# A chunked recurrence cut into five parts, with merging work behind every burst

## The chip, the cores and the metric
One Trainium2 chip, one core of it. The metric is device time in microseconds of one execution; the median of three runs counts. Lower is better.

## The reference, cut to what matters
Two transformer blocks run one behind the other, each with two layers, on 512 positions of 1024 channels in fp32. The change lies in the first block, whose layers have four branches, of which one is a recurrence (RWKV-7), and then merge the branches:

```python
def step(state, inp):                      # for each of 512 positions, 8 heads of 64
    r_t, w_t, k_t, v_t, a_t, b_t = inp
    sa = jnp.einsum('bhvk,bhk->bhv', state, a_t)
    state = (state * w_t[:, :, None, :] + sa[..., None] * b_t[:, :, None, :]
             + v_t[..., None] * k_t[:, :, None, :])
    return state, jnp.einsum('bhvk,bhk->bhv', state, r_t)
...
branches = jnp.stack([y_rwkv, y_mla, y_conv, y_mem], axis=2)
proj = jnp.einsum('bsnc,ncd->bsnd', branches, w_o_branch[l])
gates = jax.nn.sigmoid(merge.reshape(B, S, N_BRANCH, D) + b_gate[l])
merged = jnp.sum(gates * proj, axis=2)
out = merged @ w_out[l]
x = _layer_norm(DEEPNORM_ALPHA * x + out, ln_g[l], ln_b[l])
```

The second block needs modulation vectors, a product of a vector with a 1024 x 6144 matrix for each of its layers (`w_ada`). VectorE computes it in the background, the one for layer 0 during the first block's recurrences, the one for layer 1 during the second block's first feed-forward.

## The kernel before, in words
Every large product is three matmuls of 512 columns on split weights (a high and a low part, `wh` and `wl`): high by high, high by low, low by high. Weights come in 512 KB pieces on SyncE's (SP's) DMA queue into two staging buffers (`wst`), and ScalarE (cast, line 204) and VectorE (subtraction, line 181) split them. The modulation's pieces (line 1270) use the same two staging buffers and the same queue.

**The recurrence** (`rwkv`) works on four pairs of heads (j), each in two halves (g) of four chunks of 64 positions: eight units u = 2j + g in a layer. For a pair, `prep` makes r, k, v and the decays (three products of 24 matmuls each, and small ones). For a unit, `solve` makes the triangular matrices of its chunks (AB, AK, by products of AR and BK), inverts them, and transposes BK. The inversion takes the 8x8 diagonal blocks through HBM into another layout (`tri`, `BL`), inverts them by substitution on VectorE (`sub`, 14 small operations), takes them back through HBM (into `stk`, lines 653 and 661) and then doubles the block size in three levels. A level is a product with AD, an evacuation into X under a mask, a product with X, an addition and a transposition (lines 676 to 699). `chain` then runs through the four chunks one after another: z from the state, two half copies of z into `rbd` (VectorE, then ScalarE, lines 722 and 723), a product with AB, two half copies into `ubd`, a product with BT that gives the next state (`sbd`), and a product with AB that gives the output. Behind every pair the output is normalized and gated.

**The order.** All three are generators, and `together` steps the chain of unit u, the solve of unit u + 1 and, for g = 0, the prep of pair j + 1 side by side in nine rounds. Between the steps `spread` issues the filler: units of merging work (`merge`, `gates`) of the other three branches and the gates of the first, 280 units a layer. Of 24 output blocks each takes 24 matmuls for its gate in eight units and 12 for its projection in a ninth; 8 further gates take 24 matmuls in eight units. `tick2` (once a round) advances the modulation by one step, which is four VectorE operations on half a piece for one of two vectors. The generator for layer 0 (`ada(0)`) has 120 steps.

What the text issues is a list; a planner in the framework turns it into one fixed order for each engine's queue when the program is built, by its own estimate of when operands and buffers are ready, with the text's order as priority. Weight loads are moved ahead in it. On the chip each queue then runs in its fixed order, and an instruction that waits holds what stands behind it on its engine. SP's queue holds the weight loads and the DMAs of `tri`, `BL` and `stk`.

Of the kernel before, what the change touches and what calls it, by code (L numbers as in the profile page):

```python
# [19 lines left out]
P = 128  # L20
KB, PB, VB, QB, A2, NF = 3, 6, 1, 3, 4, 2
RW = 1, 2
# [8 lines left out]
TW = (0.4, 1.4) + (1,) * 7  # L31
SHARE = {1: (1,), 2: (0.5, 0.5), 3: (0.5, 0.4, 0.1)}
W0 = 0.85
# [96 lines left out]
class K:  # L130
# [386 lines left out]
    def rwkv(self, l, st):  # L517
# [19 lines left out]
        for t in (*sbd, rbd, ubd, *vbd, BK, lora):  # L537
            nc.gpsimd.memset(t, 0.0)
# [71 lines left out]
        def solve(j, g):  # L610

            col = lambda v: cv[:, v + j:v + j + 1]
            r, k, v, Pd, Pi, pc, th, kk, bon = pre[j]
            bon = bon[:, 256 * g:256 * g + 256]
            r, k, v, Pd, Pi, th, kk = [t[:, 256 * g:256 * g + 256] for t in (r, k, v, Pd, Pi, th, kk)]
            pc = pc[:, 4 * g:4 * g + 4]
            AR = pool.tile([P, 4, 2, C], F32, name="AR", tag="AR", bufs=2)
            self.tt(AR[:, :, 0, 1:C], ch(kk)[:, :, 1:C], ch(Pd)[:, :, 0:C - 1], ALU.mult)
            nc.vector.tensor_copy(out=AR[:, :, 0, 0:1], in_=ch(kk)[:, :, 0:1])
            self.stt(kk, th, 1.0, kk, ALU.add, ALU.mult)  # L620
# [3 lines left out]
            self.tt(AR[:, :, 1, :], ch(r), ch(Pd), ALU.mult)  # L624
# [4 lines left out]

            AB, AK = [pool.tile([P, 4, P], F32, name=e, tag=e, bufs=2) for e in ("AB", "AK")]  # L630
            for e, t in enumerate((AB, AK)):
# [6 lines left out]
            d1, d2 = [t[g] for t in self.tri]  # L638
            for h in range(2):
                nc.sync.dma_start(out=d1[4 * h:4 * h + 4, 0:4096].rearrange("u (k i) -> k u i", k=C),  # L640
                                  in_=AB[hd[h], :, 0:64])
            BL = pool.tile([8 * C // NB, NB, NB], F32, name="BL", tag="BL")
            nc.sync.dma_start(out=BL, in_=diag(d1))
            AD = W("AD").rearrange("p (c m) -> p c m", c=4)
            nc.gpsimd.memset(AD, 0.0)
            for b in range(4):
                nc.scalar.copy(out=AD[blk[b], :, blk[b]], in_=A1(b, b % 2, b % 2))
            for i in range(1, NB):
                t = sub[1][:, 0:i, 0:i]
                self.tt(t, sub[0][:, 0:i, 0:i].rearrange("p k q -> p q k"),  # L650
                        BL[:, 0:i, i].unsqueeze(1).to_broadcast([8 * C // NB, i, i]), ALU.mult)
                nc.vector.tensor_reduce(out=sub[0][:, i, 0:i], in_=t, axis=AX.X, op=ALU.add)
            nc.sync.dma_start(out=diag(d2), in_=sub[0])


            stk = pool.tile([P, 2, 4, 32], F32, name="stk", tag="stk")
            T, TT = stk[:, 0], stk[:, 1]
            flat = lambda t: t.rearrange("p c d -> p (c d)")
            src = d2[:, 0:4096].rearrange("(h c) (k i) -> h k c i", h=2, k=C)
            for b in range(4):  # L660
                nc.sync.dma_start(out=T[blk[b]], in_=src[b // 2, blk[b % 2], :, blk[b % 2]])
            nc.vector.transpose(out=flat(TT), in_=flat(T))
            yield
# [9 lines left out]
            for e in range(2):  # L673
                for h in hd:
                    nc.scalar.copy(out=vb[h, :, e, h], in_=ps[hd[e], :, h])
            for lv in range(L0, 5):
                if lv == 4:
                    for b in range(4):
                        nc.scalar.copy(out=A1(b, b % 2, b % 2), in_=TT[blk[b]])
                        if b % 2:  # L680
                            nc.gpsimd.memset(T[blk[b]], 0.0)
                        else:
                            nc.scalar.copy(out=AD[blk[b], :, blk[b + 1]], in_=A1(b, 0, 1))
                ps = self.psum([P, 4, 32], "tp")
                for c in range(4):
                    self.mm(ps[:, c, :], AD[:, c, :], T[:, c, :], True, True)
                X = self.tmp.tile([P, S], F32, name="X", tag="t", bufs=self.tb).rearrange(
                    "p (c b d) -> p c b d", c=4, b=4)
                self.tt(X, ps.unsqueeze(2).to_broadcast([P, 4, 4, 32]),
                        lvl[:, lv - L0:lv - L0 + 1].to_broadcast([P, 4, 4, 32]), ALU.mult)  # L690
                ps = self.psum([P, 4, 32], "tp")
                for c in range(4):
                    self.mm(ps[:, c, :], X[:, c].rearrange("p b d -> p (b d)"), TT[:, c, :], True, True)
                if lv == 4:
                    for b in (0, 2):
                        nc.scalar.copy(out=A1(b, 0, 1), in_=ps[blk[b]])
                else:
                    self.tt(TT, TT, ps, ALU.add)
                    nc.vector.transpose(out=flat(T), in_=flat(TT))
                if lv == L0:  # L700
                    bk = BK.rearrange("p c a b -> p c (a b)")
                    self.tt(bk, bk, pc.to_broadcast([P, 4, 2 * P]), ALU.mult)
                    BT = pool.tile([P, 2, 4, P], F32, name="BT", tag="BT", bufs=2)
                    for e in range(2):
                        ps = self.psum([P, 4, P], "aux")
                        for q in range(4):
                            self.tr(ps[:, q, :], BK[:, q, e, :])
                        nc.scalar.copy(out=BT[:, e], in_=ps)
                yield
            solved[j, g] = AR, AB, AK, BT, pc  # L710

        def chain(j, g):


            col = lambda v: cv[:, v + j:v + j + 1]
            AR, AB, AK, BT, pc = solved[j, g]
# [8 lines left out]
            for q in range(4):  # L725
                c = 4 * g + q
                S0, S1 = sbd[c % 2], sbd[(c + 1) % 2]
                z = self.psum([P, P], "yb")
                self.mm(z, AK[:, q, :], vbd[g][:, q, :], True, c == 0)
# [4 lines left out]
                nc.scalar.copy(out=y, in_=z[64:128, :])  # L734
                ps = self.psum([P, P], "aux")
                self.mm(ps, AB[:, q, :], rbd, True, True)
                heads(ubd, ps)
                if c < NCH - 1:
                    ps = self.psum([P, P], "aux")
                    self.mm(ps, BT[:, 1, q, :], vbd[g][:, q, :], True, False)  # L740
                    self.mm(ps, BT[:, 0, q, :], ubd, False, True)
                    for b in hd:
                        if c:
                            self.stt(S1[b, b], S0[b, b], pc[b, q, :], ps[b, b], ALU.mult, ALU.add)
                        else:
                            nc.vector.tensor_copy(out=S1[b, b], in_=ps[b, b])
                ps = self.psum([P, P], "aux")
                self.mm(ps, AB[:, q, :], ubd, True, True)
                self.tt(y, ps[64:128, :], y, ALU.add)
                yield  # L750
                if q % 2:
                    yield
            if g == 0:
                return
# [1202 lines left out]
```

## Time and profile before

| | us |
|---|---|
| median of three runs | 3342.94 (3341.34 to 3352.66) |
| the profiled execution | 3355.74, span 3354.0 |
| TensorE matmul, busy | 3178.3 (95%) |
| VectorE, busy | 2295.1 (68%) |
| ScalarE, busy | 1272.6 (38%) |
| DMA | 310 MB, 92 GB/s in the mean |

Times in the rows count from the span's start. Matmuls are pipelined, so that their recorded durations overlap, and busy TensorE time is not time at its peak; the distance from one start to the next shows the pace. An fp32 product is recorded as two matmuls. The granted clock (PEclk) is the share of TensorE's full 2.4 GHz.

### The profile page before, as it was taken

The page shows a single profiled execution, that of the slowest core. Times are in us where ns is not written, and L with a number is a line of the kernel's source. Part 1 is how long each engine was busy: PE and PEld are TensorE (multiplying, and loading weights), DVE is VectorE, ACT ScalarE, POOL GpSimd, SP SyncE. Part 2 cuts the span into 40 slices and gives each one's busy share as a digit, 9 for nine tenths or more (in the row PEclk, how much of TensorE's full clock was granted, in tenths as well). Part 3 has the DMA queues.
Part 4 walks back from the last instruction along what each step waited for, and adds up shares of the span by engine and source line. Part 5 has one row for each costly group of instructions (what it writes and reads, how often), then busy time and mean ns, then how long its engine had stood idle before and what let it go on. Part 6 is the DMA issues. An engine that isn't in the chain of part 4 may idle for free.

```text
span 3354.0 us, 44202 instructions
## 1 busy us (share of the span) xinstructions
PE 3178.3 (95%) x16694; PEld 2658.2 (79%) x16694; DVE 2295.1 (68%) x4788; ACT 1272.6 (38%) x2300; POOL 98.0 (3%) x220
## 2 busy tenths in 40 slices
PE   8999899989999998999999899999999998999999
PEld 7877677777898776787778786888888887688887
DVE  8978678776779785776647878775464667964342
ACT  4445333332344462333433457422121234732221
POOL 0000000000000010000000000000000000000000
PEclk9999899988999998999989899999999999999999
DMA  5322233323453222333224321233242442123332
GB/s 174 89 65 62 81 89 91 111 70 94 145 147 82 56 65 70 97 86 81 60 66 126 113 75 43 90 109 111 83 125 89 145 124 88 43 76 93 102 95 88
DMA packets 438661, 310.06 MB, mean 92 GB/s; under 512 B 69025, under 2 KB 430545, under 8 KB 438449
## 3 DMA queue, kind: packets, MB, share of 16 engines
q1 hardware_dynamic: 431392, 292.60, 30.2%
q0 software_dynamic: 7056, 14.65, 1.7%
q8 instruction: 131, 2.15, 0.3%
q14 instruction: 82, 0.66, 0.1%
HBM read 295.13 MB, written 7.34 MB: 90 GB/s over the span
## 4 chain that ended last, share of the span: by engine, by line
PE 48%; DVE 9%; DMA 4%; ACT 3%; issue 1%; SPq 0%; ACTq 0%; POOL 0%; DVEq 0%
PE ps_mm L192 39%; PE ps_tp L192 2%; DVE wl L181 2%; PE ps_o L192 2%; DMA wst<-in_w_in_dram 1%; ACT wh L204 1%; PE ps_sc L192 1%; DMA wst<-in_w_gate_up_dram 1%; PE ps_aux L192 1%; DVE aacc L189 1%; PE ps_mx L192 1%; PE ps_yb L192 0%; DVE z L181 0%; PE ps_mx L196 0%; DVE h8l L189 0%
## 5 line engine op out<-in xcount | busy, mean ns | idle before, releaser
L204 ACT CAST wh<-wst 128x1024 fp32r<-128x1024 f32 (+3 forms) x453 | 458.6, 1013 | 1073.0 <-PE ps_mm L192 600.3
L181 DVE TENSOR_TENSOR wl<-wst,wh 128x1024 fp32r<-128x1024 f32 (+3 forms) x453 | 532.1, 1175 | 396.0 <-ACT wh L204 388.4
L192 PE MATMUL ps_mm<-xh,wh 128*128 128x512 f32 (+1 forms) x1200 | 497.3, 415 | 15.2 <-DVE rbd L722 3.8
L192 PE MATMUL ps_mm<-xl,wh 128*128 128x512 f32 (+1 forms) x1200 | 485.8, 405 | 0.0
L192 PE MATMUL ps_mm<-xh,wl 128*128 128x512 f32 (+1 forms) x1200 | 485.2, 405 | 0.0
L192 PE MATMUL ps_mm<-h8h,wh 128*128 128x512 f32 (+1 forms) x928 | 359.3, 388 | 6.6 <-ACT wh L204 4.9
L192 PE MATMUL ps_mm<-h8l,wh 128*128 128x512 f32 (+1 forms) x928 | 358.3, 387 | 0.1
L192 PE MATMUL ps_mm<-h8h,wl 128*128 128x512 f32 (+1 forms) x928 | 356.5, 385 | 2.0 <-DVE wl L181 2.0
L192 PEld LDWEIGHTS ps_mm<-xh,wh 128*128 128x128 f32 (+1 forms) x1200 | 231.6, 193 | 66.7 <-issue 5.7
L192 PEld LDWEIGHTS ps_mm<-xh,wl 128*128 128x128 f32 (+1 forms) x1200 | 230.8, 192 | 48.3 <-issue 0.7
L192 PEld LDWEIGHTS ps_mm<-xl,wh 128*128 128x128 f32 (+1 forms) x1200 | 231.5, 193 | 43.4 <-issue 0.7
L189 DVE SCALAR_TENSOR_TENSOR aacc<-wst,silc,aacc 128x256 f32<-128x256 f32 x560 | 250.2, 478 | 15.6 <-DMA wst<-in_w_ada_dram 11.3
L192 PEld LDWEIGHTS ps_mm<-h8h,wl 128*128 128x128 f32 x928 | 175.6, 189 | 39.1 <-DVE wl L181 3.6
L192 PEld LDWEIGHTS ps_mm<-h8h,wh 128*128 128x128 f32 x928 | 176.1, 190 | 28.6 <-ACT wh L204 6.1
L192 PEld LDWEIGHTS ps_mm<-h8l,wh 128*128 128x128 f32 x928 | 175.9, 190 | 20.5 <-DVE h8l L189 0.3
L192 PE MATMUL ps_mm<-fh,wl 128*128 128x512 f32 (+1 forms) x528 | 187.0, 354 | 2.1 <-DVE wl L181 2.1
L192 PE MATMUL ps_mm<-fl,wh 128*128 128x512 f32 (+1 forms) x528 | 187.7, 356 | 0.0
L192 PE MATMUL ps_mm<-fh,wh 128*128 128x512 f32 (+1 forms) x528 | 187.3, 355 | 0.0
L189 DVE SCALAR_TENSOR_TENSOR cacc<-ch,vec,cacc 128x512 f32<-128x512 f32 x240 | 168.6, 745 | 2.3 <-ACT cacc L178 1.8
L189 DVE SCALAR_TENSOR_TENSOR ft<-ft,ps_mm 128x512 f32<-128x512 f32 (+1 forms) x134 | 76.1, 586 | 115.3 <-PE ps_mm L192 66.3
L192 PE MATMUL ps_mm<-hch,wl 128*128 128x256 f32 x448 | 127.1, 284 | 1.5 <-DVE wl L181 1.5
L192 PE MATMUL ps_mm<-hcl,wh 128*128 128x256 f32 x448 | 126.7, 283 | 0.1
(547 smaller groups left out, 6456.1 us busy)
## 6 DMA issues: line engine op xcount, KB each, us to landing
wst<-in_w_in_dram SPq DMA_DIRECT2D x188, 512.0 KB, 3.9
wst<-in_w_ada_dram SPq DMA_DIRECT2D x96, 512.0 KB, 3.6
wst<-in_w_gate_up_dram SPq DMA_DIRECT2D x88, 512.0 KB, 3.9
wst<-in_w_out_dram SPq DMA_DIRECT2D x40, 512.0 KB, 3.5
wst<-in_w_down_dram SPq DMA_DIRECT2D x36, 512.0 KB, 3.4
wst<-in_w_o_branch_dram SPq DMA_DIRECT2D x32, 512.0 KB, 3.6
wst<-in_xattn_w_mem_kv_dram SPq DMA_DIRECT2D x16, 512.0 KB, 3.6
wst<-in_w_down_dram SPq DMA_DIRECT2D x20, 384.0 KB, 3.3
```

Of the source, the lines that this page charges most:

```text
L181: return self.nc.vector.tensor_tensor(out=out, in0=a, in1=b, op=op)
L189: return self.nc.vector.scalar_tensor_tensor(out=out, in0=a, scalar=s, in1=b, op0=op0, op1=op1)
L192: self.nc.tensor.matmul(out, lhsT=l, rhs=r, start=start, stop=stop)
L204: self.nc.scalar.copy(out=h, in_=src)
```

## The change
`solve` becomes four generators (or functions), and the output's normalization a fifth part of its own, `close`. A unit now runs: `triangles` of the next unit (5 bursts), the `chain` of this one (4 chunks of 3 bursts), and `doubling` of the next (3 levels of 4 bursts). The `substitute` step comes at the chain's third burst, the next `prep` at every second burst of the chain, `operands` of the unit after next at every second burst of the doubling, and `close` at every third. Behind every burst stands a `spot` of a weight (0.8 where a prep runs beside, 1.35 elsewhere), which issues filler through `drip` at a fixed rate, 280 units over a total weight of 281.95, and every second spot calls `tick2`. A layer has 248 spots.

Within the parts: doubling works on two pairs of chunks by turns; its last level has a tile AO of its own, instead of changing AD; AD and AO last, and are cleared once. X shares the buffer of `mx` instead of the temporaries; the square and the gate of `close` move to the temporaries. In the chain the product of BT with v is issued before the AB product, and the AK product with v of the next chunk at the end of this one. The modulation's generator yields once for both vectors, except in layer 0.

```diff
+    def drip(self, w):
+        self.debt += self.rate * w
+        while self.debt >= 1:
+            self.debt -= 1
+            self.tick()
...
-        def solve(j, g):
+        def operands(j, g):
...
+        def triangles(j, g):
...
             for e, t in enumerate((AB, AK)):
...
+                if e == 0:
+                    for h in range(2):
+                        nc.sync.dma_start(out=d1[4 * h:4 * h + 4, 0:4096].rearrange("u (k i) -> k u i", k=C),
+                                          in_=AB[hd[h], :, 0:64])
+                    nc.sync.dma_start(out=BL, in_=diag(d1))
+                yield
...
+        def substitute(j, g):
...
+            nc.sync.dma_start(out=diag(d2), in_=sub[0])
+            src = d2[:, 0:4096].rearrange("(h c) (k i) -> h k c i", h=2, k=C)
+            for b in range(4):
+                nc.sync.dma_start(out=stk[blk[b], 0], in_=src[b // 2, blk[b % 2], :, blk[b % 2]])
+
+        def doubling(j, g):
...
+            two = [slice(2 * i, 2 * i + 2) for i in range(2)]
+            for s in two:
+                nc.vector.transpose(out=flat(TT[:, s]), in_=flat(T[:, s]))
             for lv in range(L0, 5):
...
+                X = W("X", "mx").rearrange("p (c b d) -> p c b d", c=4, b=4)
+                for s in two:
+                    ps = self.psum([P, 2, 32], "tp")
+                    for c in range(2):
+                        self.mm(ps[:, c, :], (AO if lv == 4 else AD)[:, s.start + c, :], T[:, s.start + c, :], True, True)
+                    self.tt(X[:, s], ps.unsqueeze(2).to_broadcast([P, 2, 4, 32]),
+                            lvl[:, lv - L0:lv - L0 + 1].to_broadcast([P, 2, 4, 32]), ALU.mult)
+                    yield
+                for s in two:
+                    ps = self.psum([P, 2, 32], "tp")
...
+                        self.tt(TT[:, s], TT[:, s], ps, ALU.add)
+                        nc.vector.transpose(out=flat(T[:, s]), in_=flat(TT[:, s]))
+                    yield
...
+        def spot(w):
+            self.drip(w)
+            spots[0] += 1
+            if spots[0] % 2:
+                self.tick2()
+
+        def turns(w, main, *side):
+            for _ in main:
+                spot(w)
+                for t in side:
+                    next(t, None)
+            for t in side:
+                for _ in t:
+                    spot(w)
...
         for _ in prep(0):
-            self.spread(W0)
-        together(W0, solve(0, 0))
+            spot(0.5)
+        for _ in operands(0, 0):
+            pass
+        turns(1, triangles(0, 0))
+        for _ in operands(0, 1):
+            pass
+        for _ in range(4):
+            spot(2)
+        substitute(0, 0)
+        for _ in range(4):
+            spot(2)
+        turns(1, doubling(0, 0))
         for u in range(8):
...
             if u < 7:
+                turns(w, triangles(*nxt))
+                turns(w, chain(j, g), after(2, substitute, *nxt), *([every(2, prep(j + 1))] if more else []))
+                side = [every(2, operands((u + 2) // 2, (u + 2) % 2))] if u < 6 else []
+                turns(w, doubling(*nxt), *side, *([every(3, close(j))] if g else []))
+            else:
+                turns(w, chain(j, g))
+                turns(w, close(j))
...
-                    yield
+                    if l == 0 or v == vecs[-1]:
+                        yield
```

## Rows read from the trace of the kernel before

**Rows 1.** The page, the chain of waits by engine.
```profile
PE 48%; DVE 9%; DMA 4%; ACT 3%; issue 1%; SPq 0%; ACTq 0%; POOL 0%; DVEq 0%
```
**Rows 2.** Windows: stretch, length, busy (count) of PE, PEld, DVE, ACT, POOL, PEclk, DMA.
```profile
318.00:852.00 534.00, 484.17 (x2415) 402.24 (x2414) 383.42 (x998) 184.01 (x391) 13.26 (x39) 0.91 0.32 92
...
1252.00:1774.00 522.00, 486.55 (x2403) 403.41 (x2402) 326.36 (x836) 182.77 (x391) 13.04 (x38) 0.91 0.28 78
```
**Rows 3.** Waits of TensorE, 318 to 852: us in total, times, longest.
```profile
PE ps_tp L192 <- DMA stk<-tri: 18.6, 4, 9.5
PE ps_tp L192 <- DVE X L181: 5.3, 7, 1.2
PE ps_aux L192 <- ACT rbd L723: 3.7, 4, 2.1
PE ps_aux L196 <- DVE sub L181: 3.4, 1, 3.4
PE ps_tp L192 <- DVE stk L699: 2.6, 2, 1.8
```
**Rows 4.** Waits of TensorE, 1252 to 1774.
```profile
PE ps_tp L192 <- DMA stk<-tri: 11.6, 2, 9.5
PE ps_tp L192 <- DVE X L181: 7.3, 8, 1.6
PE ps_tp L192 <- DVE stk L699: 2.7, 3, 1.0
```
**Rows 5.** Windows at low clock (sums of six each), and the stretch between two.
```profile
sum 92.20, PE 69.11 PEld 60.08 DVE 44.58 ACT 20.94 POOL 2.51; mean PE 11.52 PEld 10.01 DVE 7.43 ACT 3.49 POOL 0.42
...
1366.30:1376.50 10.20, 10.18 (x39) 9.31 (x39) 4.35 (x13) 3.10 (x8) 0.00 (x0) 0.50 0.13 45
...
sum 88.70, PE 74.32 PEld 65.88 DVE 38.06 ACT 18.45 POOL 2.51; mean PE 12.39 PEld 10.98 DVE 6.34 ACT 3.07 POOL 0.42
...
386.60:475.40 88.80, 84.76 (x469) 71.21 (x468) 75.86 (x208) 33.65 (x77) 2.50 (x6) 1.00 0.36 101
```
**Rows 6.** TensorE in order of time: start, us, instruction.
```profile
384.24 0.63 PE L192 MATMUL ps_mm<-xh,wl 128*128 128x512 f32 x1
384.66 0.63 PE L192 MATMUL ps_mm<-xh,wh 128*128 128x512 f32 x1
...
396.00 0.48 PE L192 MATMUL ps_mm<-xh,wh 128*128 128x512 f32 x1
396.32 0.39 PE L192 MATMUL ps_mm<-xl,wh 128*128 128x512 f32 x1
396.55 0.39 PE L192 MATMUL ps_mm<-xh,wl 128*128 128x512 f32 x1
```
**Rows 7.** First substitution, first doubling product; a round of the chain.
```profile
365.09 0.15 DVE L181 TENSOR_TENSOR sub<-sub,BL 64x1 f32<-64x1 f32 x1
...
373.43 1.89 PE L192 MATMUL ps_tp<-stk,AD 128*128 128x32 f32 x8 [9.55 <-DMA stk<-tri]
...
714.29 0.49 PE L192 MATMUL ps_yb<-sbd,AR 128*128 128x128 f32 x2 [0.34 <-DVE sbd L189]
715.82 0.38 PE L192 MATMUL ps_aux<-rbd,AB 128*128 128x128 f32 x1 [1.04 <-ACT rbd L723]
```
**Rows 8.** VectorE: X by line, a tick, modulation in the second layer, its busiest stretch.
```profile
L181 DVE TENSOR_TENSOR X<-ps_tp,lvl 128x512 f32<-128x512 f32 x24 | 16.6, 691 | 31.3 <-PE ps_tp L192 31.0
...
342.07 1.92 DVE L189 SCALAR_TENSOR_TENSOR aacc<-wst,silc,aacc 128x256 f32<-128x256 f32 x4
...
1252.00:1774.00 522.00, 57.08 (x136) 0.91 0.28 78
...
1252.00:1774.00 522.00, 11.80 (x24) 0.91 0.28 78
...
84.00:168.00 84.00, 82.62 (x141) 1.00 0.34 88
```
**Rows 9.** Waits of TensorE, 2180 to 2690, in the second block's first feed-forward.
```profile
PE ps_mm L192 <- ACT wh L204: 4.9, 3, 2.1
```

More of the change, by code (lines that the diff above doesn't have):

```diff
@@ L536, in rwkv @@
         lora = pool.tile([P, 2, P], F32, name="lora")
-        for t in (*sbd, rbd, ubd, *vbd, BK, lora):
+        AD, AO = [pool.tile([P, 4, P], F32, name=e) for e in ("AD", "AO")]
+        stk = pool.tile([P, 2, 4, 32], F32, name="stk")
+        for t in (*sbd, rbd, ubd, *vbd, BK, lora, AD, AO):
             nc.gpsimd.memset(t, 0.0)
@@ L635, in solve @@
                 self.tt(t, ps, self.m_am.unsqueeze(1).to_broadcast([P, 4, P]), ALU.mult)
-            A1 = lambda b, q, e: AB[blk[b // 2 * 2 + q], :, blk[e]]
[L638 to L645, printed above, removed]
+                if e == 0:
[4 more added lines that the diff above has]
+                yield
+            A1 = lambda b, q, e: AB[blk[b // 2 * 2 + q], :, blk[e]]
             for b in range(4):
                 nc.scalar.copy(out=AD[blk[b], :, blk[b]], in_=A1(b, b % 2, b % 2))
[L648 to L662, printed above, removed]
-            yield
+                if b % 2 == 0:
+                    nc.scalar.copy(out=AO[blk[b], :, blk[b + 1]], in_=A1(b, 0, 1))
             self.stt(r, r, col(V_RK), k, ALU.mult, ALU.mult)
@@ L679, in solve @@
                         nc.scalar.copy(out=A1(b, b % 2, b % 2), in_=TT[blk[b]])
[L680 to L708, printed above, removed]
@@ new lines, in doubling @@
+                for s in two:
+                    ps = self.psum([P, 2, 32], "tp")
+                    for c in range(2):
+                        self.mm(ps[:, c, :], X[:, s.start + c].rearrange("p b d -> p (b d)"), TT[:, s.start + c, :],
+                                True, True)
+                    if lv == 4:
+                        for b in (0, 2):
+                            nc.scalar.copy(out=A1(b, 0, 1)[:, s], in_=ps[blk[b]])
+                    else:
+                        self.tt(TT[:, s], TT[:, s], ps, ALU.add)
+                        nc.vector.transpose(out=flat(T[:, s]), in_=flat(TT[:, s]))
+                    yield
@@ L734, in chain @@
                 nc.scalar.copy(out=y, in_=z[64:128, :])
+                if not last:
+                    pb = self.psum([P, P], "aux")
+                    self.mm(pb, BT[:, 1, q, :], vbd[g][:, q, :], True, False)
+                yield
                 ps = self.psum([P, P], "aux")
@@ L777, in chain @@
             yield
-        def together(w, *gs):
-            gs = list(gs)
-            for i in range(9):
-                live = list(gs)
-                for q, t in enumerate(live):
-                    if next(t, 0) == 0:
-                        gs.remove(t)
-                    self.spread(w * TW[i] * SHARE[len(live)][q])
-                self.tick2()
-                if not live:
-                    self.spread(w * TW[i])
-            for t in gs:
-                for _ in t:
-                    pass
@@ new lines, in every, with after @@
+        def every(n, t):
+            for i, _ in enumerate(t):
+                yield
+                for _ in range(n - 1):
+                    yield
+        def after(n, f, *args):
+            for _ in range(n):
+                yield
+            f(*args)
+            yield
+        pre, ops, solved = {}, {}, {}
+        self.rate = self.units / RWT
+        self.debt = 0.0
+        for _ in prep(0):
+            spot(0.5)
+        for _ in operands(0, 0):
+            pass
+        turns(1, triangles(0, 0))
@@ L799, in rwkv @@
+        for _ in operands(0, 1):
[6 more added lines that the diff above has]
+        turns(1, doubling(0, 0))
         for u in range(8):
             j, g = u // 2, u % 2
-            gs = [chain(j, g)]
+            more = g == 0 and j < 3
+            w = RWW[0] if more else RWW[1]
+            nxt = (u + 1) // 2, (u + 1) % 2
             if u < 7:
-                gs.append(solve((u + 1) // 2, (u + 1) % 2))
```

102 lines of the change are left out of this document (61 added, 41 removed).

## The prediction, made before the changed kernel was run

> **What bounds the kernel now.** I read the page's chain of waits first. Its largest part by far is TensorE, 48% of the span and nothing else over 9% [rows 1]: the kernel is a stream of 512-column matmuls against streamed weights, and time is lost only where that stream stops or runs at half clock. So I went to the windows by stage. The recurrence stands in two stretches, 318 to 852 us (first layer) and 1252 to 1774 us (second). In both the granted clock averages 0.91 and TensorE is busy some 91 and 93% of the time by a measure that counts overlapping ends [rows 2]. Third, I asked whom TensorE waits for there. The longest waits are not the recurrence's products but a DMA: the inverted 8x8 blocks, which go to HBM and back (stk<-tri), cost 18.6 us in the first stretch and 11.6 in the second. Next come the doubling's own round trips (X and the transposes at line 699), 7.9 and 10.0 us. Behind the small substitution on VectorE (sub), itself behind another DMA, 3.4 us are lost, and in the chain 3.7 us behind the copies to rbd in the first layer [rows 3, 4]. Fourth, the clock: six low stretches in each layer, 92.2 and 88.7 us at 1.2 GHz instead of 2.4, with TensorE busy for 69.1 and 74.3 us of them [rows 5]. In such a stretch a 512-column matmul takes 0.42 us from start to start, at the full clock 0.23 [rows 6]. So about half of that busy time is lost, 34.6 and 37.2 us: more than all the waits together. The longest single wait is 9.55 us for stk and ends at 373.43; the matmuls behind it, at 384.24, run at the low clock [rows 6, 7].
>
> **The change part by part.** The sum is made against the profiled execution, 3355.7 us (span 3354.0), 12.8 us or 0.4% above the median of 3342.94. I take the difference over to the median unchanged.
>
> (a) The round trip through HBM. Before, a unit emits product, DMA out, DMA in, substitution, DMA out, DMA in and the transposition in one step with no filler inside. After, the block loads follow the first product, the substitution comes at the third burst of the chain, and its blocks are wanted after nine more bursts. From the first substitution on VectorE to the transposed blocks' first product is 365.09 to 373.43, 8.3 us [rows 7]. One unit of filler is on average 0.87 us: 280 units share 24 outputs of 24 and 12 matmuls and 8 outputs of 24, which is 1056 matmuls of 0.23 us [rows 6], 243 us. Nine spots of weight 0.8 or 1.35 are 6.3 or 10.6 us, with three products of 24 matmuls of the next head pair beside the lighter ones, and nine bursts of some 0.4 us: all longer than 8.3. Only in the first unit of a layer does filler alone stand there, four spots of weight 2, 7.0 us, and some 1.5 us may remain. Gain: 18.6 + 3.4 - 1.5 = 20.5 us in the first layer, 11.6 - 1.5 = 10.1 in the second. SP's queue still holds these DMAs in order among the weight loads: a load queued behind the write that waits for the substitution comes later by that wait, as it does before. Bounds: nothing gained, or all 33.6.
>
> (b) Doubling in pairs. Each level's two products for four chunks become four bursts for two, with filler behind each. Between a burst and the one that needs it lies the other pair's burst and two fillers, 0.4 + 2 x 0.7 us at least, against single waits that are now at most 1.8 us [rows 3, 4]. I take three quarters of 7.9 and 10.0: 5.9 and 7.5 us. Bounds: 0 and all. The splitting costs VectorE: X over 512 columns is 0.691 us, four operations on 256 columns take 1.92 [rows 8], so 24 halvings a layer cost at most 24 x (2 x 0.48 - 0.691) = 6.5 us, and the halved additions and transposes between nothing and as much again; I take 8 us in all (bounds 0 and 13), which the filler hides as long as VectorE is no bound. AD and AO become lasting tiles, so the memsets on GpSimd and at the last level go; nothing on the path waited long for them, and I count nothing.
>
> (c) The chain alone. Before, steps of the chain and of the next solve alternate; after, a chunk's three bursts have only filler, every second spot a part of the next preparation, and four matmuls that were moved ahead of need (the BT and AK products with v) between them. A round through the two head copies is 714.29 to 715.82, 1.53 us with 1.04 of it waiting [rows 7]. The filler of 0.7 to 1.2 us plus the moved 0.2 us covers that roughly. VectorE must serve these copies in order, and a tick of the modulation work is four operations, 1.92 us [rows 8]. I put (c) at 0. Bounds: a gain of the 3.7 us behind rbd [rows 3] and as much again behind the other copies; a loss of that 1.04 us at each of 192 bursts, 200 us, if nothing covered them.
>
> (d) The clock. The low stretches follow waits of (a) and (b). The stretch between the first layer's first two, 386.6 to 475.4, ran at 2.4 GHz throughout with TensorE busy 84.8 of 88.8 us, though bursts and filler alternated in it [rows 5]. That is the state that the change spreads over the whole recurrence. I take three quarters of the loss: 26 and 28 us. Bounds: 0 and 72.
> The Trainium skill speaks against this term. "TensorE: Matmul & The Clock Gate", section "A second HAM failure mode: psum-queue depth-cycling", says that many short idles between groups of matmuls, with no long one among them, are enough to make the clock swing. By that rule twice as many bursts, each ending in an evacuation, would keep the 72 us lost and the sum would lose all of (d). One low stretch bears it out: 1366.3 to 1376.5 is at 1.2 GHz with TensorE busy 10.18 of 10.20 us [rows 5], and no wait over 1.6 us for X is recorded in its layer [rows 4].
>
> (e) Switches. The first filler matmul behind a burst takes 0.32 us to the next, 396.00 to 396.32, where others take 0.23 [rows 6]. There are 248 spots a layer; if some 110 of them are new switches, 110 x 0.09 = 10 us a layer. Bounds 0 and 22.
>
> (f) The modulation's ticks. Before, nine ticks in each of nine rounds make 81 a layer, and the generator of 120 steps runs into the second layer; there its operations take VectorE 57.1 + 11.8 us [rows 8]. After, every second of 248 spots ticks, 124 a layer: all of it falls into the first. VectorE there goes from 383.4 to 383.4 + 68.9 + 8 = 460 us, in the second from 326.4 to 265 [rows 2, 8]. Without this the first stretch would shrink by 20.5 + 5.9 + 26 - 10 = 42, to 492 us, and VectorE would have to be busy 94% of it. The best it does in the trace is 82.62 of 84 us, in work that waits for nobody [rows 8]; in the recurrence it is 72%. I take 90%, nearer to the first because the added operations wait only for their DMA: 460 / 0.9 = 511 us, a cost of 19. Bounds: 0 (98%) and 49 (85%, 541 us, a little worse than now).
>
> (g) In the second block's feed-forward the same generator yields once for two vectors in its first eight column blocks. TensorE's longest waits there, for weights, are 4.9 us in all [rows 9]: up to 5 us either way, counted as 0.
>
> Sum: first layer 42 - 19 = 23, second 10.1 + 7.5 + 28 - 10 = 36, together 59 us: 3355.7 becomes 3297, and the median 3342.9 becomes 3284.
>
> **The rivals.**
> (1) VectorE binds the first layer outright, bound of (f): that stretch gains nothing, the second its 36: 3307 us. For it: 460 us of work in order on an engine whose results the chain awaits. Against: it is idle for 151 of the 534 us now.
> (2) The clock doesn't recover: without (d) the first stretch gains 16, with VectorE then at 89% and no cost, the second 8: 3343 - 24 = 3319 us. For it: the low stretch from 1366.3. Against: the 88.8 us at full clock.
> (3) Slower: the chain, now alone, waits in most of its 192 bursts. Its place is z to rbd to AB and ubd to BT on TensorE's queue; its price is the round of 1.5 us less the filler of weight 0.8, about 0.6, and up to another 1.9 where four modulation operations stand before the copies on VectorE. It decides from a mean of 59 / 192 = 0.3 us a burst; at 0.5 us it is 96 - 59 = 37 us slower, 3380. Against: the waits for rbd are few now, four in the whole first stretch [rows 3], and the planner can issue other work before its place in the text. The Trainium skill has the queue side of it, "TensorE: Matmul & The Clock Gate", section "Architectural detail: the array is 16× 32×32, not 1× 128×128": VectorE's queue is strictly first in, first out. The trace's 1.92 us run of modulation work [rows 8] is what that rule would put ahead of a copy; no row here shows it happening.
> (4) It doesn't do what it says: the planner orders each queue by its own times and takes the text's order as priority alone. If its order comes out much as before: 3343 us. For it: nothing in the text kept it from putting filler into the 9.55 us wait [rows 7], and it didn't. Against: no filler stood in the text at that place.
>
> **How the numbers follow.** The forecast has 0.49, rival (1) 0.17, (2) 0.13, (3) 0.13, (4) 0.08. The predicted time is the likeliest one's, 3284 us. Its own range, from half of (d) and (b) lost to (f) free and all of (a), (b) and (d) gained, is 3240 to 3318. The range to hold it 8 times in 10 reaches from 3235 past rivals (1) and (2) to 3350, which leaves out most of (3). A change under 0.3%, 10 us, can't be told from none here. Faster by more: nearly all of the forecast, of (1) and of (2) and a third of (4), 0.75; within: 0.09; slower: (3) and a third of (4), 0.16.
>
> **What would show it.** (a) right: TensorE's wait for stk<-tri falls from 30.2 to under 5 us in both layers together. (b): waits for X and the doubling's transposes under 6 us. (c) wrong: waits for rbd, ubd and sbd over 30 us a layer. (d) right: under 50 us at 1.2 GHz in both recurrences instead of 181; wrong if over 120. (f) right: no modulation work in the second layer's recurrence, VectorE over 88% busy in the first, and the first stretch shortened less than the second. The prediction as a whole is wrong if the second layer's stretch, which has nothing of (f), isn't shorter by at least 15 us.

## The result, and the profile after

The changed kernel takes 3269.57 us (median of four, 3265.71 to 3273.42) against 3347.23 (3341.34 to 3352.66) for the kernel before beside it: a ratio of 0.9768, 95% interval 0.9743 to 0.9793. The forecast was 3284. That the size is so close is partly luck: errors of both signs met in the sum, as the stretches show.

Each profiled span is cut at the same events: a recurrence runs from the first value of its low-rank gate (wlal) to the first cast of the closing merge (mgh).

| stretch, us | before | after | difference | forecast |
|---|---|---|---|---|
| up to the first recurrence | 323.2 | 326.2 | +3.0 | 0 |
| first recurrence | 555.5 | 535.5 | -20.0 | -23 |
| between | 377.5 | 377.4 | -0.1 | 0 |
| second recurrence | 546.4 | 470.1 | -76.3 | -36 |
| behind | 1551.4 | 1561.1 | +9.7 | 0 |
| span | 3354.0 | 3270.3 | -83.7 | -59 |

The windows of the two recurrences and of what is behind them in the changed kernel, columns as in [rows 2] with GB/s last:

```profile
326.20:861.70 535.50, 493.25 (x2503) 404.25 (x2502) 453.80 (x1233) 194.06 (x417) 3.22 (x7) 0.96 0.39 112
1239.10:1709.20 470.10, 467.85 (x2520) 387.87 (x2519) 289.43 (x787) 192.73 (x419) 5.48 (x11) 1.00 0.28 76
1709.20:3270.30 1561.10, 1494.74 (x8095) 1261.86 (x8093) 967.01 (x1831) 555.50 (x919) 29.88 (x55) 0.99 0.32 94
```

The same windows of the kernel before, cut at its events:

```profile
323.20:878.70 555.50, 505.28 (x2507) 419.18 (x2506) 400.02 (x1033) 191.81 (x402) 10.10 (x29) 0.92 0.33 94
1256.20:1802.60 546.40, 510.95 (x2512) 423.18 (x2511) 343.71 (x866) 190.89 (x402) 14.13 (x37) 0.92 0.30 82
```

In the second recurrence TensorE is now busy almost without a break: at full clock throughout, with 2.25 us not busy where it was 35.45. Of the 76.3 us, 33.2 are waits and 43.1 busy time. By the prediction's own measure, half of the busy time at low clock [rows 5], the clock accounts for 37.2 of the 43.1; the other 5.9 weren't taken apart. The first recurrence gained 8.0 us of waits and 12.0 of busy time. It keeps 42 us not busy, and eight stretches at 1.2 GHz, together:

```profile
sum 47.60, PE 39.60 PEld 32.88 DVE 35.27 ACT 13.57 POOL 0.00; mean PE 4.95 PEld 4.11 DVE 4.41 ACT 1.70 POOL 0.00
```

Whom TensorE waits for in the changed kernel, first recurrence (us, times, longest):

```profile
PE ps_mm L197 <- ACT wh L209: 16.8, 13, 4.0
PE ps_aux L197 <- ACT ubd L745: 5.6, 6, 3.4
PE ps_aux L197 <- ACT rbd L745: 5.1, 6, 3.0
PE ps_tp L197 <- DVE stk L732: 3.9, 3, 3.1
PE ps_tp L197 <- DVE X L186: 2.3, 1, 2.3
```

and the whole list of the second:

```profile
PE ps_aux L197 <- ACT rbd L745: 1.0, 1, 1.0
PE ps_mm L197 <- ACT tg L183: 0.6, 2, 0.4
```

The wait for the inverted blocks from HBM [rows 3, 4] is in neither list, nor in the rest of the first. At the head of the first there now stands a wait for the cast of a streamed weight (wh), which was 1.0 us there before. The new order on TensorE can be read in order of time (start, us, instruction), here a doubling level of the second layer:

```profile
1288.19 0.97 PE L197 MATMUL ps_tp<-stk,AD 128*128 128x32 f32 x8
1288.99 0.48 PE L197 MATMUL ps_mm<-xh,wh 128*128 128x512 f32 x1
1289.31 0.39 PE L197 MATMUL ps_mm<-xl,wh 128*128 128x512 f32 x1
1289.54 0.40 PE L197 MATMUL ps_mm<-xh,wl 128*128 128x512 f32 x1
1289.77 0.53 PE L197 MATMUL ps_tp<-stk,X 128*128 128x32 f32 x4
1290.13 0.47 PE L197 MATMUL ps_mm<-xh,wh 128*128 128x512 f32 x1
1290.45 0.53 PE L197 MATMUL ps_tp<-stk,X 128*128 128x32 f32 x4
```

No line has a wait: small products and 512-column matmuls alternate. Counted over the second recurrence, the 512-column matmuls on streamed weights (those into ps_mm) stand in 222 runs where there were 135, and the longest stretch without one went from 24.0 us, waits included, to 2.8.

### The profile page after: what moved, and what is told of

It is laid out like the page before. It is cut to its first block, busy times and chain, and to the rows that moved or that the text cites. A ratio compares the mean times of both kernels' runs of the same rounds, so it can differ in the third digit from the quotient of the medians.

```text
span 3270.3 us, 44267 instructions
## 1 busy us (share of the span) xinstructions
PE 3126.8 (96%) x16694; PEld 2610.3 (80%) x16694; DVE 2300.7 (70%) x4916; ACT 1276.8 (39%) x2332; POOL 85.3 (3%) x176
## 4 chain that ended last, share of the span: by engine, by line
PE 49%; DVE 8%; DMA 3%; ACT 3%; issue 1%; SPq 0%; ACTq 0%; POOL 0%; DVEq 0%
PE ps_mm L197 40%; PE ps_o L197 2%; PE ps_tp L197 2%; DMA wst<-in_w_gate_up_dram 2%; DVE wl L186 2%; PE ps_aux L197 1%; PE ps_sc L197 1%; ACT wh L209 1%; DVE aacc L194 1%; DMA wst<-in_w_in_dram 1%; PE ps_mx L197 1%; PE ps_yb L197 1%; DVE n2t L194 0%; DVE z L186 0%; DMA wst<-in_w_ada_dram 0%
## 5 line engine op out<-in xcount | busy, mean ns | idle before, releaser
L197 PE MATMUL ps_mm<-xh,wh 128*128 128x512 f32 (+1 forms) x1200 | 499.7, 417 | 20.8 <-ACT wh L209 16.8
L197 PE MATMUL ps_mm<-h8h,wh 128*128 128x512 f32 (+1 forms) x928 | 360.6, 390 | 14.0 <-ACT wh L209 12.4
```

Of the source, the lines that this page charges most:

```text
L197: self.nc.tensor.matmul(out, lhsT=l, rhs=r, start=start, stop=stop)
```

## The experiments

Ratios are to the kernel before on the same chip. Stretches come from one profile each: two kernels below that run the same code up to the end of the second recurrence (the first and the third) have 478.8 and 488.4 us for it, so a stretch is good to some 10 us.

**The modulation shared by both recurrences.**

```diff
-            if spots[0] % 2:
+            if spots[0] % 4 == 1:
```

> The edit: a modulation step at one of four spots instead of one of two, so the 120 steps of the modulation are shared by the two recurrences (62 spots each) and no longer all fall into the first. Theory M (the modulation is what keeps the first recurrence long: 535.5 us with the changed kernel against 470.1 us for the second, with 330 products into aacc and 47 pieces of 512 KB loaded there): the first recurrence becomes 20 to 45 us shorter, its low-clock time falls from 47.8 us to under 25, the second becomes 0 to 12 us longer, total 15 to 40 us faster than the changed kernel (3230 to 3255 us). Rival N (the first recurrence is long because of what lies beside it otherwise: its own gate weights and the attention results): the first stays within 5 us of 535, total within 5 us of 3269.6. Rival O (what the first gains the second loses one for one): 3265 to 3275 us with the second near 500 us.

Measured: 3221.59 us, ratio 0.963 (0.9602 to 0.9657). First recurrence 474.3, second 478.8:

```profile
327.10:801.40 474.30, 469.19 (x2509) 388.59 (x2508) 372.82 (x1015) 193.19 (x419) 3.26 (x7) 1.00 0.35 101
1182.10:1660.90 478.80, 471.89 (x2520) 390.91 (x2520) 367.91 (x999) 192.75 (x418) 5.36 (x11) 0.99 0.35 99
```

M held and was too small: 61.2 us gained in the first, more than its 45, and 8.7 lost in the second. With all the modulation the first recurrence had eight low stretches and 42 us of waits; with half it has no low stretch and 5.1 us not busy.

**The generator's pauses as before.**

```diff
-                    if l == 0 or v == vecs[-1]:
-                        yield
+                    yield
```

> The edit: the modulation generator pauses after each vector again, as before the change; for the first layer this is the same number of steps (120), for the second layer's modulation 88 thinner steps instead of 72 thicker ones. Theory: the 9.7 us that the changed kernel loses behind the two recurrences (1551.4 to 1561.1 us, arising as +14.4 us in the two-stream feed-forward) come from the thicker steps: the feed-forward becomes 8 to 14 us shorter, nothing else moves by more than 3 us, total 3256 to 3263 us. Rival: the loss comes from another place (the queue of the weights, or where the second recurrence's end leaves the clock): total within 4 us of 3269.6.

Measured: 3254.09 us, ratio 0.973 (0.9705 to 0.9754); behind the recurrences 1546.0 us, 15.1 shorter, the recurrences 531.7 and 469.2. The place is the first eight outputs of the two-stream feed-forward, whose windows are, after and in this run (before: also 126.3):

```profile
2105.30:2246.10 140.80, 126.53 (x695) 108.65 (x694) 106.91 (x228) 29.12 (x46) 0.00 (x0) 0.98 0.44 131
```

```profile
2105.10:2231.40 126.30, 122.06 (x679) 106.08 (x678) 82.07 (x168) 28.41 (x44) 0.00 (x0) 0.97 0.37 112
```

The wait of TensorE for the cast of weights in these windows, after and in this run:

```profile
PE ps_mm L197 <- ACT wh L209: 12.2, 6, 3.8
```

```profile
PE ps_mm L197 <- ACT wh L209: 3.6, 2, 2.0
```

So step (g) costs 15.1 us, and some 5 us gained elsewhere behind the recurrences leave the +9.7: each pause now carries eight products and the pieces come faster, 131 GB/s against 112, into a place whose weights have little slack.

**Both.** 

> Both edits at once: a modulation step at one of four spots instead of one of two, and the pause after each vector again. Theory: the two act in different stretches (the first gave 61.2 us in the first recurrence and took 8.7 in the second; the second gave 15.1 us in the second block), so they add: first recurrence 470 to 478 us, second 474 to 482, behind them 1543 to 1549; total 3203 to 3211 us, ratio to before about 0.959. Rival: with the modulation's thinner steps the weights' queue meets another load and the second block gives less than 5 of its 15 us: 3214 to 3222 us.

Measured: 3214.35 us, ratio 0.959 (0.9563 to 0.9616); first 477.4, second 488.4, behind 1547.9. The total is 3 us above the theory's range, inside the rival's, but the rival's condition isn't met: behind the recurrences 13.2 of the 15.1 us are gained. So they add, apart from the scatter of the second recurrence (20.5 us at low clock, where the first run had 6.8).

**What of the modulation hurts: no loads, then fewer products.** Without loads (the products read the constant tile ident in place of the weights, so the modulation by the weights is left out):

```diff
-                nc.sync.dma_start(out=st, in_=src.rearrange("(k p) c -> p k c", p=P))
+                if l:
+                    nc.sync.dma_start(out=st, in_=src.rearrange("(k p) c -> p k c", p=P))
...
+                        sv = st[:, k, :] if l else self.ident.unsqueeze(1).to_broadcast([P, 2, P])
...
```

> The edit: the first layer's modulation reads a constant tile that lies in memory instead of its weights; its 48 pieces are not loaded and hold no staging buffer. The same number of VectorE operations on as many elements stays (left out: the modulation by the weights). It parts two reasons for the waits of the first recurrence (535.5 us, 40 us of it TensorE waiting). T1 (the pieces hold the two staging buffers and SP's queue, so the gate weights come late: ScalarE's cast waits 62.1 us for them there, TensorE 16.8 us for the cast): first recurrence 475 to 500 us, low-clock time under 20 us. T2 (VectorE, 453.8 us busy of 535.5, is itself late with what the recurrence needs): first recurrence 525 to 540 us with VectorE still some 450 us busy.

With fewer products (the second vector's are left out):

```diff
-                    for k in range(4):
+                    for k in range(4) if l or v == 0 else ():
...
```

> The edit: the first layer's modulation does its products for one vector of two (192 of 384 products left out, some 0.45 us each; the modulation of the second vector is therefore not computed) but loads every piece as before. The mirror of the run with no loads. T1 (staging buffers and SP's queue): the pieces are freed somewhat sooner, first recurrence 515 to 535 us with VectorE 375 us busy. T2 (VectorE's own load): first recurrence 475 to 505 us, low-clock time under 25 us.

Measured, one run each: 3227.13 and 3221.37 us; first recurrences 497.9 us without loads, 493.2 with half of the products.

```profile
324.80:822.70 497.90, 477.24 (x2509) 393.49 (x2508) 445.82 (x1227) 193.49 (x419) 3.37 (x7) 0.99 0.25 72
```

```profile
325.30:818.50 493.20, 479.43 (x2508) 396.91 (x2508) 392.42 (x1047) 193.33 (x419) 3.19 (x7) 0.98 0.42 122
```

ScalarE's cast waits for gate weights from HBM, first in the changed kernel, then without loads, then with half of the products:

```profile
ACT wh L209 <- DMA wst<-in_w_in_dram: 47.7, 27, 5.1
```

```profile
ACT wh L209 <- DMA wst<-in_w_in_dram: 15.8, 9, 4.1
```

```profile
ACT wh L209 <- DMA wst<-in_w_in_dram: 27.4, 18, 5.1
```

By its ranges the first run bears out T1 and the second T2, so neither theory holds alone: taking away either half gains 37.6 or 42.3 of the 61 to 65 us that lie between this stretch and one with half or none of the modulation. Each shortens ScalarE's wait, and TensorE's wait for the cast falls from 16.8 us to 0.7 and 3.1. A likely reason, argued and not tested by itself, is the two staging buffers, in which the two halves meet: a piece of the modulation holds one for eight products of VectorE. VectorE's load alone doesn't explain the stretch: without the loads it was busy 445.8 of 497.9 us, 90%, in less time. It isn't free either, since that stretch is still 23.6 us longer than with half of the modulation.

**Substitution called late, and doubling with four chunks at once.**

```diff
-                turns(w, chain(j, g), after(2, substitute, *nxt), ...)
+                turns(w, chain(j, g), ...)
+                substitute(*nxt)
```

> The edit undoes one part: the substitution with its DMA round trip is called right before the doubling, no longer after two bursts of the chain. Read in the second recurrence, which has no modulation work (470.1 us, TensorE waiting 2.3 us). Theory A (the early start hides the round trip): the waits of TensorE for stk from HBM return, 2 to 5 us at each of 8 units, 15 to 40 us, and with them some low clock: second recurrence 490 to 520 us. Rival B (merging work behind every burst covers it wherever it stands, or the order on the engines is made by readiness): second recurrence 468 to 476 us, no such wait over 2 us in all. In the first recurrence, loaded with the modulation, A gives the same and more: 545 to 580 us.

```diff
+            two = [slice(0, 4)]
...
-                    ps = self.psum([P, 2, 32], "tp")
-                    for c in range(2):
+                    ps = self.psum([P, 4, 32], "tp")
+                    for c in range(4):
...
                     yield
+                    yield
```

> The edit undoes one part: the doubling takes its four chunks at once (one multiplication into X instead of two, and so on: 24 operations on VectorE fewer in a layer for X alone), with as many spots for merging work as before, two of them in a row. Theory A (the pairs hide one half's product behind the other's copy): second recurrence 5 to 15 us longer than 470.1, with waits of TensorE for X and for the transposes of 5 to 12 us. Rival B (the merging work hides that as well, and the pairs only cost VectorE operations): second recurrence 466 to 472, first recurrence 3 to 10 us shorter than 535.5, since VectorE is the loaded engine there.

> Two parts undone at once, the substitution called right before the doubling and the doubling with all four chunks at once; the merging work stays behind every burst. Each alone left the second recurrence where it was (469.7 and 469.3 us against 470.1). Theory F (the merging work behind every burst is what covers, so neither part is needed): second recurrence 467 to 476 us without low clock, first 525 to 548. Rival R (each of the two parts covers for the other): second recurrence 485 us or more, with waits of TensorE for stk or X over 8 us.

Measured: ratios 0.9782 (0.9758 to 0.9806) and 0.9742 (0.9721 to 0.9764); both undone, one run, 3259.48 us. The second recurrence is the same in all three, in that order:

```profile
1249.10:1718.80 469.70, 467.65 (x2520) 388.04 (x2520) 289.46 (x787) 192.53 (x419) 5.51 (x11) 1.00 0.29 76
```

```profile
1238.20:1707.50 469.30, 467.75 (x2520) 387.65 (x2520) 285.38 (x723) 190.42 (x403) 5.49 (x11) 1.00 0.29 76
```

```profile
1231.60:1700.70 469.10, 467.25 (x2520) 387.72 (x2518) 285.27 (x723) 190.22 (x402) 5.46 (x11) 1.00 0.27 76
```

The first recurrences took 542.3, 531.7 and 528.3 us. So the pairs are worth nothing here, and B and F held. The late call tells less than it was meant to. In the second recurrence, from the last sum of a substitution to the first product on its blocks it is 7.5 to 19.3 us with 30 to 62 matmuls of 512 columns between, and with the early call 7.1 to 20.3 us with the same 30 to 62. The planner put the substitution at the same place in both, so this call's place in the text isn't what sets it; the product and the block loads ahead of the chain, which no run undid, may be. In the kernel before it was 5.6 to 7.9 us with 0 to 25 matmuls.

**No merging work behind the bursts.** What would be issued there comes in one lump at the end of each unit.

```diff
         def spot(w):
-            self.drip(w)
+            held[0] += w
...
+            held[0] = 0.0
...
                 turns(w, doubling(*nxt), ...)
...
+            self.drip(held[0])
```

> The edit keeps the new parts and their order but issues no merging work behind the bursts: what would be issued there is held back and issued in one lump at the end of each of the eight units. Theory A (the merging work behind every burst is what covers the waits): second recurrence 520 to 620 us, with waits of TensorE for rbd, ubd, sbd and X of 50 us and more and low clock of 50 us and more. Rival B (the order on the engines is made by readiness and not by the place in the text): second recurrence 468 to 480 us.

> The same two parts undone, and the merging work issued in one lump at the end of each unit. With the lump alone the second recurrence took 503.8 us (the kernel before: 546.4). Theory D (without cover behind each burst the early round trip and the pairs are worth what the prediction gave them, some 10 and 7 us a layer, and the clock with them): second recurrence 520 to 550 us, waits for stk from HBM 8 us or more. Rival E (they are worth nothing there either; what is left between 503.8 and 546.4 us comes from the order of the parts within the chain and from the modulation that left the layer): second recurrence 497 to 512 us.

Measured: 3370.68 us, ratio 1.0054 (1.0037 to 1.0072), half a per cent slower than the kernel before; with both other parts undone too, one run, 3368.09 us. The second recurrences, lump, then lump with both undone:

```profile
1296.00:1799.80 503.80, 488.65 (x2525) 403.37 (x2524) 291.88 (x791) 192.18 (x419) 6.47 (x13) 0.96 0.27 73
```

```profile
1298.10:1813.70 515.60, 495.95 (x2524) 408.46 (x2523) 288.97 (x727) 190.32 (x403) 6.38 (x13) 0.94 0.26 71
```

The first recurrences took 591.3 and 595.2 us. For the lump, neither A (520 or more) nor B (480 or less) has the second recurrence right: the planner still draws part of the lump forward (156 runs of 512-column matmuls against 222), but not enough. For the second kernel neither D nor E does; no wait for the blocks from HBM over 1 us came back, against D, and 11.8 us between the two is about the scatter. What the lump costs against the changed kernel, 33.7 us, and with both parts undone 515.6 against 469.1, 46.5 us, is well beyond it. TensorE's waits for X and for the doubling's transposes are 2.3 us with the lump and 6.4 with the pairs undone as well, against 10.0 before and none in the changed kernel: without merging work behind each burst the pairs may help a little.

The lump shows what goes before the clock's falls. All three low stretches of its second recurrence begin in a stretch in which small products, with short waits between them, stand without a 512-column matmul. One such stretch, the low one that starts in it, and the wait before that start:

```profile
1551.30:1559.00 7.70, 5.46 (x31) 4.91 (x30) 7.33 (x23) 2.64 (x4) 0.00 (x0) 0.69 0.14 47
1554.30:1568.00 13.70, 11.99 (x43) 10.45 (x43) 7.94 (x27) 4.55 (x14) 0.00 (x0) 0.50 0.27 78
...
1553.22 1.20 PE L197 MATMUL ps_tp<-stk,AD 128*128 128x32 f32 x8 [0.48 <-DVE stk L186]
```

**The kernel before with all modulation in its first recurrence.** Two steps a round instead of one:

```diff
                 self.tick2()
+                self.tick2()
```

> The kernel before with two modulation steps a round instead of one, so that all 120 fall into its first recurrence and none into its second, as in the changed kernel. It prices, without the new order, the modulation that left the second recurrence (546.4 us with it). Theory P (it is small there: half of the modulation added 8.7 us to the second recurrence of the changed kernel): second recurrence 532 to 545 us, first 570 to 600 instead of 555.5. Rival Q (it is most of what lies between 546.4 us and the 515.6 us that are left with the lump and both parts undone): second recurrence 512 to 526 us.

Measured, one run: 3388.79 us beside 3349.5; recurrences of 601.6 (a little over P's range) and 532.5 us, so P. Without its modulation, the old order's second recurrence is still 62 us longer than the new one's.

```profile
323.90:925.50 601.60, 519.00 (x2500) 426.25 (x2499) 455.03 (x1177) 190.90 (x401) 10.10 (x29) 0.90 0.36 100
1304.60:1837.10 532.50, 504.56 (x2512) 416.64 (x2511) 293.22 (x722) 191.53 (x403) 14.20 (x37) 0.93 0.26 69
```

**The best.** Shared modulation, the old pauses, doubling with four chunks at once.

> A candidate: modulation at one of four spots, the pause after each vector, and the doubling with four chunks at once (64 VectorE operations fewer in a layer than with the pairs). If the pairs are worth nothing under the merging work and VectorE still matters a little in both recurrences: first recurrence 468 to 478 us, second 470 to 488, total 3196 to 3212 us, ratio to before 0.953 to 0.959. Rival (the pairs matter where VectorE is 78% busy): second recurrence over 490 us, ratio over 0.962.

Measured: 3205.57 us, ratio 0.9569 (0.9543 to 0.9594), recurrences 472.3 and 476.6, all within the theory's ranges: 4.3% under the kernel before, and about 2% under the changed one by the two ratios. Against 0.959 with the pairs kept it can't be told apart.

## Why the prediction was right, step by step

The two orders can be compared with a like placing of the modulation:

| us | old order, first + second | new order, first + second | gain |
|---|---|---|---|
| modulation shared | 555.5 + 546.4 | 474.3 + 478.8 | 148.8 |
| all in the first | 601.6 + 532.5 | 535.5 + 470.1 | 128.5 |

The second row has the same placing in both orders. In the first row the old order has some 82 of the 120 steps in the first recurrence and the new one 60, so the 148.8 is not the order alone. The new order is thus worth some 128 to 149 us, 1.6 to 1.9 times the forecast's gain before (f), 78. Moving the modulation into the first recurrence takes back 52.5 of it in the new order (61.2 less 8.7, from 60 steps) and 32.2 in the old (46.1 less 13.9, from 82). The prediction had both signs right and both sizes too small.

The lump belongs into this comparison, since all its modulation is in the first recurrence too: its recurrences take 591.3 + 503.8, 39.0 us less than the old order's in the second row and 89.5 more than the new order's. So by these profiles, one each, some 90 of the 128.5 us need the merging work behind the bursts, and some 39 come with the other parts of the change, which weren't separated further.

(a) Right by its sign: the wait for stk from HBM fell from 30.2 us to none. It was 0.4 us with a late call in each recurrence, and not over 2 us with the lump; what it needs of the new order wasn't separated further.

(b) The waits are gone in the second layer, and 6.2 us are left in the first (X and the transposes of L732), a little over the 6 that were named. But the cause is wrong in one half: four chunks at once do as well, so the merging work between the bursts is enough, and the pairs that the term was named for add nothing to it. Their waits were a part only: everything else that TensorE waited for in the second recurrence went as well, 33.2 us in all against the 17.6 forecast by (a) and (b) in that layer.

(c) Right: rbd, ubd and sbd together cost 12.4 us in the first layer and 1.0 in the second, not 30. The chain alone is covered. Rival (3) isn't borne out even without that cover: the lump, its nearest test, takes 3370.68 us, less than the 3388.79 of the old order with the same placing of the modulation.

(d) Right in its sign, mis-sized in both layers: 47.6 us at low clock are left in the first and none in the second, under the 50 that were named, of 181. In the second all of the 37.2 us came back, not 28. In the first the 39.6 us of busy time still at low clock cost 19.8, so 14.8 of the 34.6 came back, not 26. What spoke against the term falls. The low stretch at 1366.3 [rows 5] begins at the end of a wait of 1.48 us for X, behind 5.8 us (from 1362.2) without a matmul into ps_mm:

```profile
1362.66 1.02 PE L192 MATMUL ps_aux<-wlal,lora 128*128 128x512 f32 x2
...
1366.32 1.92 PE L192 MATMUL ps_tp<-stk,X 128*128 128x32 f32 x8 [1.48 <-DVE X L181]
1368.05 0.77 PE L192 MATMUL ps_mm<-yh,wh 128*128 128x512 f32 x1
```

The prediction read that stretch by itself, in which TensorE is busy, and not what stands before it. All six low stretches of that recurrence in [rows 5] begin in stretches of 5.8 to 24.0 us without a matmul into ps_mm (a seventh, of 3.4 us, does not). Such a stretch has both waits and small products in it, and no run parts the two.

The Trainium skill, "TensorE: Matmul & The Clock Gate", section "A second HAM failure mode: psum-queue depth-cycling", tells of a bf16 kernel in which frequent short idles between groups of matmuls were enough to make the clock swing. The second recurrence doesn't test that, since TensorE idled for only 2.25 us in it; the low stretches of the lump and the one at 1366.3, which begin behind idles of 0.48 and 1.48 us, don't speak against it. What failed is the step from more bursts to more idles: with 222 runs of matmuls between small products in place of 135, the clock never fell.

(e) Wrong: no loss to switches shows. The second recurrence's busy time, 467.85 us at full clock, is under what the kernel before would have had without its loss to the clock, 510.95 - 37.2 = 473.8. The 0.32 us behind a burst are still there (1288.99 to 1289.31 above), but they are no loss. Eight small products and the 512-column matmul behind them take 1.12 us (1288.19 to 1289.31), four and one take 0.68 (1289.77 to 1290.45). So a small product takes 0.11, and the 512-column matmul adds 0.24, about the 0.23 that it takes behind another one [rows 6].

So the second layer's forecast of 36 misses 40 us: 15.6 in waits, 25 in (d) less (e). A part of it is a term that the prediction put at nothing there: the modulation that left. In the old order that is 13.9 us (546.4 to 532.5).

(f) Right in kind, mis-sized: VectorE's work came about as forecast (453.8 us for 460), no modulation is left in the second recurrence, and the first gained less than the second. The term was 19 us, at most 49, for some 39 more steps. The old order paid 46.1 for these; the new order paid 61.2 against a kernel with 60 steps. The failing step is the measure: a busy share of VectorE, 90% taken and 85% found. The share isn't the mechanism, as 90% was reached without the loads. The gate weights came late too, TensorE waited (16.8 us for the cast), and the clock fell. The first layer's -20.0 for -23 is two errors that cancel: against the run with half of the modulation 81 us were gained, some of them by its fewer steps, and 61 lost, for 42 and 19. That is luck.

(g) Counted as nothing, with up to 5 us either way, it cost 14.5 us in its place and 15.1 by the end of the span, as the run with the old pauses shows. [rows 9] showed a wait of 4.9 us for the cast of weights; it is 12.2 us now in the first eight outputs alone. What was read as little to lose was a place with little slack.

Rival (1) was nearest of the others: the first layer is held up, but by loads and VectorE together. Rival (4) is right about one edit, the place of the substitution's call, and wrong of the change: where the merging work stands in the text decides 33.7 us of the second recurrence.

## What to carry to other kernels

Put independent 512-column work behind every burst of small products of a serial chain, in the text too; here the waits alone were less than half of what the change brought in the second recurrence (33.2 of 76.3 us), mostly because the clock came back with them. With this cover a finer trick on the same waits, the pairs, added nothing. Filler for another engine that also loads can't be priced by that engine's busy share alone: its loads and the slack of the place that it lands in counted here as well, and sharing it between both recurrences gained 52.5 us. Before you call a piece of a change the cause, compare runs with the same placing of everything else: the lump looks slower than the kernel before, and is 39 us faster in the recurrences once the modulation stands alike.

## What the hardware showed that was not expected

VectorE, 85% busy, and a stream of loads together held up TensorE: taking away half of the products or all of the loads gained 42.3 and 37.6 us of some 61. And a recurrence in which 222 runs of 512-column matmuls alternate with bursts of small products ran 470 us without a drop of the clock; with four chunks at once it was 186 runs and no drop either. In the second recurrences of the kernel before and of the three runs that lost clock there without modulation, the drops of 10 us and more began in stretches of 5.8 to 24.9 us without a matmul on streamed weights, in which small products and waits stood.
